# Ninth gate and up pair of a gated MLP as seven block products, with its weight sums formed in DRAM

## The chip, the cores and the metric

The kernel runs on one core of one Trainium2 chip. The metric is the device time of one execution in microseconds (us); the time before is 644.41 us, the median of three runs (644.31 to 644.88). The engines named below are TensorE (PE in the profile, with its weight loads as PEld), VectorE (DVE), ScalarE (ACT), GpSimd (POOL), and SyncE (SP), whose queue issues most transfers.

## The reference

One decoder layer on 512 tokens of width 1024: forgetting attention with 16 heads, a layer norm, a gated MLP, a second layer norm and a gated embedding. Only the MLP matters here:

```python
def conv_ffn(x, w_up, conv_w, conv_b, w_down):
    u, g = jnp.split(x @ w_up, [FFN_DIM], axis=-1)          # FFN_DIM = 2816
    g = causal_dwconv(g, conv_w, conv_b)                    # 3 taps along the tokens
    return (jax.nn.gelu(g, approximate=False) * u) @ w_down
```

## The kernel before

Every float32 product is made of three matmuls in a reduced float32 format. Each operand is split into a high part (a rounded copy, by ACT) and a low part (the operand less the high part, by DVE); the products high by high, high by low and low by high are summed in PSUM (`three`, line 147). The class `Weights` (line 64) holds a list of weight units of up to 128 x 1024 elements in the order of their use. A unit is loaded by the SP queue into one of four `raw` buffers (every fifth unit into a spare one), perhaps combined with other blocks by its `make` function on DVE, and then cut into its `whi` and `wlo` tiles, of which there are five of each (lines 123 and 129). `W.get(u, 4)` cuts all units up to the fourth behind `u`, so DVE and ACT receive the work on a weight four units ahead of its use.

The 2816 columns of the MLP are 22 blocks `f` of 128. Two neighbouring blocks are a pair `j`. A plain pair multiplies all eight k-blocks by all 512 tokens, for gate and up of both blocks (`up`, line 789): 4 x 8 x 3 = 96 matmuls of 512 columns. A pair in `UP_PAIRS` is treated as a 2 x 2 block product (two halves of k by the two blocks `f`, and two halves of the tokens), with seven instead of eight products (`up_step`, line 836). Its steps 0, 1, 2 and 3 hold two, two, two and one product for gate and the same for up: 7 x 2 x 4 x 3 = 168 matmuls of 256 columns. This needs sums of weight blocks. For the pairs 3 to 7 (`KEPT`) DVE forms them during attention (`keep_sums`, line 488) and they wait in DRAM tiles `kept`; for the pairs 2 and 9 the `make` functions `t12`, `t3`, `t4` (lines 199 to 226) form them when needed (line 208, 209, 216 and 224). Pair 8 is plain. Such a pair has seven weight units where a plain one has four.

The output product with `w_down` is also done by seven products, on three groups of three pairs (`down`, line 910): its generator yields after each of its 12 chunks, which are spread through the pairs of the next part by `CHUNKS` (line 32) in the calls of `between` (line 961). In phase `ua` the chunks 0, 1 and 2 use the first, second and third pair of the group before, their operands A11 and A12. When a chain is complete, `give` (line 934) adds its PSUM banks to `y` in SBUF (lines 703 and 705). The six banks of the chains (`y`, `z`, `x`, two of each) come from a pool of six; two more banks belong to another tag.

The operands of `down` come from a pair's products: `operand_sums` (line 892) forms four sums on DVE, and `operand_parts` (line 904) cuts the blocks A, B and S into high and low parts (for pair 8 the tiles `a8`, `b8`, `s8`). For a pair whose successor is in `APART` this is put off: the sums are called inside the second step 0 of the next pair (`amid`, line 865), and the parts right after that step (lines 988 to 994). Pair 8 is not in `APART`, so pair 7's operands, and pair 8's own, are made directly at the end of their pairs (line 1030). From block 2 on, `tc.manual_schedule` (line 971) fixes the order of the instructions of DVE and ACT as the code gives it. The order on PE and the queues is chosen by the framework when the program is built.

Part 3 (from line 957) holds the pairs 9 and 10. With the chunk counts (2, 1) repeated, the order of pair 9 in the code is: step 0 of gate, chunks 0 and 1, step 0 of up, chunk 2, step 1 of gate and of up, chunks 3 and 4, step 2 of both, chunk 5, step 3 of both. Beside the pairs, `gate_sums` (line 277) issues one accumulating transfer for each block from 6 on, on the POOL queue, each behind a tiny ACT copy (line 282) and a tiny POOL copy (line 283): they form the weight sums of the last gate in DRAM tiles `gt`.

Of the kernel before, what the change touches and what calls it, by code (L numbers as in the profile page):

```python
# [40 lines left out]
HALF = S // 2  # L41
ALPHA = 2.0 ** 0.25
EPS = 1e-5
# [99 lines left out]
def trunk_layer(ctx: ExitStack, tc: tile.TileContext, xT, x2d, pT, w0, wqk, wv1, wv2, bf, wo, wup, cwb,  # L143
# [10 lines left out]

    base = ctx.enter_context(tc.tile_pool(name="base", bufs=1))
    psum = ctx.enter_context(tc.tile_pool(name="psum", bufs=6, space=bass.MemoryType.PSUM))
    turns = itertools.cycle(BANKS)

    def bank(name, tag=None):

        tag = tag or next(turns)
        return psum.tile([P, 512], F32, tag=tag, name=name, bufs={"six": 6, "two": 2}[tag])

    def half_rows(w, k0, n, cols):
        return w[k0 * P:(k0 + n) * P, cols * 512:(cols + 1) * 512].rearrange("(k p) c -> p k c", p=P)
# [30 lines left out]

        return aside[0][:, i, :]

    def t12(b11, i):
        def make(t):  # L200
            if t is None:
                to = side(i)
                if len(b11.shape) == 3:
                    to = to.rearrange("p (a b) -> p a b", b=P)
                nc.sync.dma_start(to, b11)
                return None
            t1, t2 = t[:, :512], side(i)
            nc.vector.tensor_sub(t1, t1, t2)
            nc.vector.tensor_sub(t2, t[:, 512:], t1)
            return [t1, t2]  # L210
        return make

    def t3(t):
        if t is None:
            return None
        nc.vector.tensor_sub(t[:, :512], t[:, 512:], t[:, :512])  # L216
        return [t]

    def t4(i, n=2):
        def make(t):  # L220
            if t is None:
                return None
            v = t[:, :n * 512]
            nc.vector.tensor_sub(v, v, aside[0][:, i:i + n, :].rearrange("p a b -> p (a b)"))
            return [v]
        return make

# [12 lines left out]
    def up_units(j):  # L240

        f0, f1 = 2 * j, 2 * j + 1
        if j in KEPT:
# [8 lines left out]
        return (lambda q: unit(f0, q), lambda q: unit(f1, q, t12(wup[f0, 1 - q][:, :4], 3 + q)),  # L252
                lambda q: unit(f1, q, t3),
                lambda q: W.add([(wup[f0, 1 - i][:, 4:], 512) for i in range(2)], make=t4(3)))

    dram = ctx.enter_context(tc.tile_pool(name="dram", bufs=1, space=bass.MemoryType.DRAM))
    kept = {(j, q): dram.tile([P, 4, 512], F32, name=f"kept{j}_{q}") for j in KEPT for q in range(2)}


    gq = {f"t{n}": dram.tile([P, 4, 512], F32, name=f"gt{n}") for n in range(1, 5)}  # L260

    steps = itertools.count(16)

    def quad(g, k, n):
        src = gq[g] if g in gq else half_rows(wg, 4 * int(g[1]) - 4, 4, int(g[2]) - 1)
        return src[:, k:k + n, :]
# [7 lines left out]
                    nc.gpsimd.dma_start(quad(to, k, 2), quad(src, k, 2))  # L274
        yield

    def gate_sums():

        for to, src in (("t1", "b12"), ("t2", "t1"), ("t4", "t2"), ("t3", "b12")):
            for k in range(4):  # L280
                m = next(steps)
                nc.scalar.activation(small[:, m:m + 1], zeros[:, :1], AF.Copy)  # L282
                with tc.issue_after(nc.gpsimd.tensor_copy(small[:, m + 32:m + 33], small[:, m:m + 1]).ins):  # L283
                    nc.gpsimd.dma_start(quad(to, k, 1), quad(src, k, 1), accum_op=ALU.add)
                yield

    u_up, u_dn = {}, [[] for _ in PAIRS]
    for part in range(4):
# [180 lines left out]
            nc.gpsimd.memset(t[:, :P].bitcast(F32), 0.0)  # L469


    to_keep, in_work, made, last_sum, last_mask = list(kept.items()), [], [], [], []

    def keep_load(queue=nc.sync):

# [12 lines left out]
    def keep_sums(first=last_mask):  # L488

        if in_work:  # L490
            behind = ExitStack()
            if first:
                behind.enter_context(tc.issue_after(first[0]))
            to, ab = in_work.pop()
            b11, b21, b12, b22 = [t[:, c:c + 512] for t in ab for c in (0, 512)]
            nc.vector.tensor_sub(b11, b12, b11)
            nc.vector.tensor_sub(b12, b22, b12)
            nc.vector.tensor_sub(b22, b22, b11)
            last_sum[:] = [nc.vector.tensor_sub(b21, b21, b22).ins]
            behind.close()  # L500
            made.append((to, ab))

# [108 lines left out]

    outs = {}
    acc = {}

    def out_first(k):
        hi, lo = W.get(u_o[0][k // 2])
# [202 lines left out]
    def x_sums():  # L819
        def blk(t, k):  # L820
            return xt[t][:, 4 * k:4 * k + 4, :]

        def s(n, i):
            return sums[n][:, :, i * P:(i + 1) * P]

        for i in range(2):
            nc.vector.tensor_add(s(0, i), blk(2 + i, 0), blk(2 + i, 1))
            nc.vector.tensor_sub(s(1, i), s(0, i), blk(i, 0))
            nc.vector.tensor_sub(s(2, i), blk(i, 0), blk(2 + i, 0))
            nc.vector.tensor_sub(s(3, i), blk(i, 1), s(1, i))  # L830
        for n in range(4):
            k = slice(4 * n, 4 * n + 4)
            nc.scalar.activation(xs[0][:, k, :], sums[n], AF.Copy)
            nc.vector.tensor_sub(xs[1][:, k, :], sums[n], xs[0][:, k, :].bitcast(F32))

    def up_step(j, st, s, E, amid=None):
# [30 lines left out]
        elif st == 1:  # L867
            go(z, 0, True, sn=0)
            go(x, 1, True, sn=1)
            nc.scalar.activation(e[:, S:S + HALF], x, AF.Copy)  # L870
            nc.scalar.activation(e[:, S + HALF:], z, AF.Copy)
            if j in APART:
                nc.scalar.activation(e[:, :HALF], c1, AF.Copy)
        elif st == 2:
            go(z, 1, True, sn=3)
            go(x, 0, True, sn=2)
            nc.vector.tensor_add(e[:, S:], ps, e[:, S:])
# [14 lines left out]
    def operand_sums(E):  # L892


        def e(n):
            return E[:, n * HALF:(n + 1) * HALF]

        a21, a11, a22, a12, s1, s2, s3, s4 = [e(n) for n in range(8)]
        nc.vector.tensor_add(s1, a21, a22)
# [10 lines left out]
    def down(part, ops):  # L910
# [4 lines left out]
        A11, A12, A22, S1, S2, S3, S4 = (0, 0), (0, 1), (1, 0), (2, 0), (2, 1), (2, 2), (2, 3)  # L915
# [37 lines left out]
    before = None  # L953
    pending = []
    beside = gate_sums()
    ordered = ExitStack()
    for part in range(4):
        ops = []
# [5 lines left out]

        for f in range(6 * part, min(6 * part + 6, NF)):
            q, j = f % 2, f // 2
            if f >= 6:
                next(beside)
            if f == 2:

# [287 lines left out]
```

## Time and profile before

| | |
|---|---|
| time, median of three runs | 644.41 us |
| time of the profiled execution | 644.6 us |
| its span (first to last instruction) | 642.9 us |
| granted TensorE clock | 0.999 |
| PE busy | 636.6 us, 99% of the span |
| DVE busy | 540.7 us, 84% |
| ACT busy | 389.4 us, 61% |
| POOL busy | 129.1 us, 20% |

A row of the timeline gives the start in us, the duration, the engine, the line of the code, the operation and its output and inputs; idle time ahead of it stands in brackets with what ended it. A row of the chain of work gives start, duration, engine, the output's name and the number of instructions. A row of the windows gives for a stretch of time its length, then the busy time of PE, PEld, DVE, ACT and POOL with their instructions, the granted clock, the share of DMA time and GB/s. A row of the groups gives the count, the busy time and the mean in ns, and the idle time before. In the chain, `g` and `u` are gate and up, and `x`, `y`, `z` chains of the output product.

### The profile page before, as it was taken

Reading aid. Unit: us, or ns where it says so; the run is one execution under the profiler, and the core shown is the slowest. Engines: PE = TensorE matmul, PEld = TensorE weight load, DVE = VectorE, ACT = ScalarE, POOL = GpSimd, SP = SyncE. Lnnn points to the kernel's source line nnn. Section 1 sums busy time; section 2 is a strip of 40 time slices with the busy share of each in tenths; the row PEclk is TensorE's granted clock in tenths of the full one; section 3 lists DMA queues with packets and bytes.
Section 4 is the critical chain, followed back from the end, with each engine's and each line's share of the span. In section 5 each row is a group of like instructions: output and inputs, shape, how many; then the busy total and the mean of one; then the engine's idle time right before and its main releaser. Section 6 shows DMA issues by size and latency. Waiting matters only on the chain.

```text
span 642.9 us, 10251 instructions
## 1 busy us (share of the span) xinstructions
PE 636.6 (99%) x3707; PEld 562.4 (87%) x3707; DVE 540.7 (84%) x864; ACT 389.4 (61%) x690; POOL 129.1 (20%) x149
## 2 busy tenths in 40 slices
PE   9999999999999999999999999999999999999997
PEld 7899888888888889989999999999988998888886
DVE  7577779988888689857889989999986998599996
ACT  6273787877785316956666566756644455236872
POOL 2000464454456043110000000102020001002001
PEclk9999999999999999999999999999999999999999
DMA  8766634554588777694676868675854774662632
GB/s 316 249 225 211 220 105 166 175 193 152 181 280 295 269 258 204 147 252 137 197 224 154 239 183 275 189 234 168 255 152 123 207 246 100 181 232 73 221 108 98
DMA packets 51666, 126.87 MB, mean 197 GB/s; under 512 B 5088, under 2 KB 8160, under 8 KB 51616
## 3 DMA queue, kind: packets, MB, share of 16 engines
q1 hardware_dynamic: 46384, 111.93, 52.1%
q0 software_dynamic: 5088, 14.16, 11.3%
q8 instruction: 29, 0.48, 0.3%
q14 instruction: 21, 0.17, 0.1%
q10 hardware_dynamic: 144, 0.13, 0.1%
HBM read 111.39 MB, written 20.97 MB: 206 GB/s over the span
## 4 chain that ended last, share of the span: by engine, by line
PE 92%; DVE 4%; issue 1%; DMA 1%; POOL 0%; SPq 0%; ACT 0%; DVEq 0%; POOLq 0%
PE u L152 17%; PE g L152 17%; PE pp L152 13%; PE x L152 8%; PE pl L152 7%; PE pv L152 7%; PE z L152 4%; PE r L152 3%; PE o L600 3%; PE ao L152 3%; PE t L587 3%; PE y L152 2%; PE s L550 2%; PE s L552 2%; PE p L152 1%
## 5 line engine op out<-in xcount | busy, mean ns | idle before, releaser
L123 ACT ACTIVATE whi<-raw 128x1024 fp32r<-128x1024 f32 (+4 forms) x131 | 128.9, 987 | 92.2 <-PE pv L152 18.4
L129 DVE TENSOR_TENSOR wlo<-raw,whi 128x1024 fp32r<-128x1024 f32 (+4 forms) x126 | 141.7, 1129 | 26.7 <-ACT whi L123 26.0
L574 POOL TENSOR_SCALAR pr<-pr,rl 128x128 f32<-128x128 f32 (+1 forms) x64 | 75.6, 1197 | 74.7 <-DVE rl L570 74.7
L283 POOL COPY neghalf<-neghalf 128x1 f32<-128x1 f32 x16 | 9.6, 601 | 244.3 <-ACT neghalf L282 244.3
L152 PE MATMUL g<-x1h,whi 128*128 128x256 f32 (+1 forms) x164 | 51.7, 315 | 0.0
L152 PE MATMUL g<-x1l,whi 128*128 128x256 f32 (+1 forms) x164 | 51.6, 315 | 0.0
L152 PE MATMUL g<-x1h,wlo 128*128 128x256 f32 (+1 forms) x164 | 51.5, 314 | 0.0
L152 PE MATMUL pp<-xh,wlo 128*128 128x512 f32 (+1 forms) x130 | 50.5, 390 | 0.0
L152 PE MATMUL pp<-xh,whi 128*128 128x512 f32 (+1 forms) x130 | 50.5, 388 | 0.1
L152 PE MATMUL pp<-xl,whi 128*128 128x512 f32 (+1 forms) x130 | 50.4, 388 | 0.0
L152 PE MATMUL u<-x1l,whi 128*128 128x256 f32 (+1 forms) x156 | 50.1, 321 | 0.0
L152 PE MATMUL u<-x1h,wlo 128*128 128x256 f32 (+1 forms) x156 | 50.1, 321 | 0.0
L152 PE MATMUL u<-x1h,whi 128*128 128x256 f32 (+1 forms) x156 | 50.1, 321 | 0.0
L566 ACT ACTIVATE pr<-s,nm 128x128 f32<-128x128 f32 (+1 forms) x64 | 33.6, 527 | 11.8 <-DVE nm L562 11.7
L152 PEld LDWEIGHTS g<-x1h,whi 128*128 128x128 f32 x164 | 31.2, 191 | 2.4 <-issue 0.4
L152 PEld LDWEIGHTS g<-x1l,whi 128*128 128x128 f32 x164 | 31.2, 190 | 2.1
L152 PEld LDWEIGHTS g<-x1h,wlo 128*128 128x128 f32 x164 | 31.2, 190 | 1.9
L123 ACT ACTIVATE whi<-side 128x512 fp32r<-128x512 f32 (+1 forms) x32 | 26.4, 828 | 9.3 <-DVE side L216 3.8
L152 PEld LDWEIGHTS u<-x1l,whi 128*128 128x128 f32 x156 | 29.7, 190 | 2.4
L152 PEld LDWEIGHTS u<-x1h,whi 128*128 128x128 f32 x156 | 29.7, 190 | 2.3
L152 PE MATMUL g<-xsh,wlo 128*128 128x256 f32 x112 | 31.7, 283 | 0.0
L152 PE MATMUL u<-xsh,whi 128*128 128x256 f32 x112 | 31.7, 283 | 0.0
(637 smaller groups left out, 1927.7 us busy)
## 6 DMA issues: line engine op xcount, KB each, us to landing
raw<-wup SPq DMA_DIRECT2D x30, 512.0 KB, 4.8
raw<-wdn SPq DMA_DIRECT2D x26, 512.0 KB, 4.8
raw<-wqk SPq DMA_DIRECT2D x14, 512.0 KB, 3.9
ka<-wup SPq DMA_DIRECT2D x10, 512.0 KB
kb<-wup SPq DMA_DIRECT2D x10, 512.0 KB, 4.3
kept<-kb SPq DMA_DIRECT2D x9, 512.0 KB, 3.4
kept<-ka SPq DMA_DIRECT2D x9, 512.0 KB
raw<-wo SPq DMA_DIRECT2D x8, 512.0 KB, 5.1
```

The lines of the kernel that those rows point to most:

```text
L123: self.nc.scalar.activation(hi[:, c:e], piece, AF.Copy)
L129: self.nc.vector.tensor_sub(lo[:, c:e], piece, hi[:, c:e].bitcast(F32))
L152: nc.tensor.matmul(ps, lhsT, rhs, start=start and n == 0, stop=stop and n == 2, skip_group_check=on)
L283: with tc.issue_after(nc.gpsimd.tensor_copy(small[:, m + 32:m + 33], small[:, m:m + 1]).ins):
L550: nc.tensor.matmul(ps[:, :n], QA[:, q], KA[:, :n], start=True, stop=False)
L552: nc.tensor.matmul(ps[:, :n], qb[0:68, q], kb[0:68, :n], start=False, stop=True)
L566: nc.scalar.activation(pr[:, off:off + w], ps[:, :w], AF.Exp, bias=nm[:, i:i + 1], scale=-1.0, accum_out=ls[:, i:i + 1])
L574: nc.gpsimd.tensor_scalar_mul(pr[:, off:off + w], pr[:, off:off + w], rl[:, i:i + 1])
L587: nc.tensor.transpose(ps[:, w:w + P], pr[:, o:o + P], ident)
L600: nc.tensor.matmul(ps[:, q0:], V[:, j, h], p[:, o:o + w], start=j == 0 and n == 0, stop=j == NT - 1 and n == 1)
```

## The change

Pair 8 joins `UP_PAIRS` and becomes seven products. Its weight sums are not made by DVE. Four transfers during the heads 2 and 3 copy the raw blocks to two DRAM tiles (`up_copies`, on the SP queue), and eight accumulating transfers (`sums_beside`, on the POOL queue) turn them into the sums. [...] The eight transfers come ahead of the sixteen of the last gate, one per block from 4 to 14, two from 15 to 20, one at 21 (`BESIDE`).

Pairs 8 and 9 join `APART`: the operands of pair 7 are made in the second step 0 of pair 8, and those of pair 8 in the second step 0 of pair 9. `CHUNKS` of part 2 takes the pattern of part 1, so its third pair (8) has the counts 0, 1, 2, 1 where it had 1, 1, 1, 1. The `y` chains are no longer added to `y` after every part: their two banks are kept and accumulate through three parts, and `give` adds them once. For this the pool of six banks is split in four and two, taken in the turn four, four, two. `operand_sums` does its four subtractions and sums in three operations.

```diff
-CHUNKS = (None, (1,) * 8 + (0, 1, 2, 1), (1,) * 12, (2, 1) * 4)
-UP_PAIRS = (2, 3, 4, 5, 6, 7, 9)
+CHUNKS = (None,) + ((1,) * 8 + (0, 1, 2, 1),) * 2 + ((2, 1) * 4,)
+UP_PAIRS = (2, 3, 4, 5, 6, 7, 8, 9)
+IN_DRAM = (8,)
+BESIDE = (0,) * 4 + (1,) * 11 + (2,) * 6 + (1,)
-APART = (2, 3, 4, 5, 6, 7)
+APART = (2, 3, 4, 5, 6, 7, 8, 9)
+COPIES = (2, 3)
...
-    turns = itertools.cycle(BANKS)
+    turns, sixth = itertools.cycle(BANKS), itertools.cycle(("four", "four", "duo"))
...
+        if tag == "six":
+            tag = next(sixth)
...
+    def up_copies():
+        for j in IN_DRAM:
+            for q in range(2):
+                for n in range(2):
+                    nc.sync.dma_start(kept[j, q][:, 2 * n:2 * n + 2, :].rearrange("p a (k b) -> p (a k) b", b=P),
+                                      wup[2 * j + n, 1 - q])
+                    yield
+    def sums_beside():
+        def blocks(j):
+            for to, src in ((0, None), (2, None), (3, 0), (1, 3)):
...
+        for to, src in itertools.chain(*[blocks(j) for j in IN_DRAM], gates()):
+            m = next(steps)
+            nc.scalar.activation(small[:, m:m + 1], zeros[:, :1], AF.Copy)
+            with tc.issue_after(nc.gpsimd.tensor_copy(small[:, m + 32:m + 33], small[:, m:m + 1]).ins):
+                nc.gpsimd.dma_start(to, src, accum_op=ALU.add)
+            yield
...
+        for _ in range(2 if h in COPIES else 0):
+            next(copies)
...
-        nc.vector.tensor_sub(s2, s1, a11)
-        nc.vector.tensor_sub(s3, a11, a21)
+        nc.vector.tensor_sub(e3[:, 5:7, :], e3[:, 0:5:4, :], a11.unsqueeze(1).to_broadcast([P, 2, HALF]))
         nc.vector.tensor_sub(s4, a12, s2)
...
-        acc = {(b, i): bank(f"{b}{part}{i}", "six") for b in "yzx" for i in range(2)}
-        seen, opened = set(), set()
+        acc = {(b, i): bank(f"{b}{part}{i}", "four") for b in "zx" for i in range(2)}
+        if not lasting:
+            lasting.update({("y", i): bank(f"y{i}", "duo") for i in range(2)})
+        acc.update(lasting)
+        seen, opened = set(), {("y", i) for i in range(2) if part}
...
-                        give(b, half, c)
+                        if b != "y" or part == len(PAIRS) - 1:
+                            give(b, half, c)
```

More of the change, by code (lines that the diff above doesn't have):

```diff
@@ L156, in trunk_layer @@
     psum = ctx.enter_context(tc.tile_pool(name="psum", bufs=6, space=bass.MemoryType.PSUM))
-    turns = itertools.cycle(BANKS)
+    turns, sixth = itertools.cycle(BANKS), itertools.cycle(("four", "four", "duo"))
     def bank(name, tag=None):
         tag = tag or next(turns)
-        return psum.tile([P, 512], F32, tag=tag, name=name, bufs={"six": 6, "two": 2}[tag])
+        if tag == "six":
+            tag = next(sixth)
+        return psum.tile([P, 512], F32, tag=tag, name=name, bufs={"four": 4, "duo": 2, "two": 2}[tag])
     def half_rows(w, k0, n, cols):
@@ L215, in t3, with up_t3, t4 @@
             return None
-        nc.vector.tensor_sub(t[:, :512], t[:, 512:], t[:, :512])
+        nc.vector.tensor_sub(t[:, :512], t[:, :512], t[:, 512:])
         return [t]
-    def t4(i, n=2):
+    def up_t3(t):
+        if t is None:
+            return None
+        nc.vector.tensor_add(t[:, :512], t[:, 512:], t[:, :512])
+        return [t]
+    def t4(i, n=2, op=nc.vector.tensor_sub):
         def make(t):
@@ L250, in unit @@
             return W.add(wup[f, 1 - q], inner=P, make=make, by_dma=make is None and j in DMA_PAIRS)
-        return (lambda q: unit(f0, q), lambda q: unit(f1, q, t12(wup[f0, 1 - q][:, :4], 3 + q)),
-                lambda q: unit(f1, q, t3),
-                lambda q: W.add([(wup[f0, 1 - i][:, 4:], 512) for i in range(2)], make=t4(3)))
+        add = nc.vector.tensor_add
+        return (lambda q: unit(f0, q), lambda q: unit(f1, q, t12(wup[f0, 1 - q][:, :4], 3 + q, add)),
+                lambda q: unit(f1, q, up_t3),
+                lambda q: W.add([(wup[f0, 1 - i][:, 4:], 512) for i in range(2)], make=t4(3, op=add)))
     dram = ctx.enter_context(tc.tile_pool(name="dram", bufs=1, space=bass.MemoryType.DRAM))
-    kept = {(j, q): dram.tile([P, 4, 512], F32, name=f"kept{j}_{q}") for j in KEPT for q in range(2)}
+    kept = {(j, q): dram.tile([P, 4, 512], F32, name=f"kept{j}_{q}")
+            for j in KEPT + IN_DRAM for q in range(2)}
     gq = {f"t{n}": dram.tile([P, 4, 512], F32, name=f"gt{n}") for n in range(1, 5)}
-    steps = itertools.count(16)
+    steps = itertools.cycle(range(16, 32))
     def quad(g, k, n):
@@ L275, in gate_copies, with gates @@
         yield
[L277 to L285, printed above, removed]
+    def up_copies():
[8 more added lines that the diff above has]
+            for to, src in ((0, None), (2, None), (3, 0), (1, 3)):
+                for q in range(2):
+                    t = kept[j, q]
+                    if src is None:
+                        yield (t[:, to, :].rearrange("p (k b) -> p k b", b=P),
+                               wup[2 * j + 1, 1 - q][:, 2 * to:2 * to + 4])
+                    else:
+                        yield t[:, to, :], t[:, src, :]
+        def gates():
+            for to, src in (("t1", "b12"), ("t2", "t1"), ("t4", "t2"), ("t3", "b12")):
+                for k in range(4):
+                    yield quad(to, k, 1), quad(src, k, 1)
+        for to, src in itertools.chain(*[blocks(j) for j in IN_DRAM], gates()):
[4 more added lines that the diff above has]
+            yield
     u_up, u_dn = {}, [[] for _ in PAIRS]
@@ L469, in trunk_layer @@
             nc.gpsimd.memset(t[:, :P].bitcast(F32), 0.0)
-    to_keep, in_work, made, last_sum, last_mask = list(kept.items()), [], [], [], []
+    to_keep = [(k, t) for k, t in kept.items() if k[0] in KEPT]
+    in_work, made, last_sum, last_mask = [], [], [], []
     def keep_load(queue=nc.sync):
@@ L495, in keep_sums @@
             b11, b21, b12, b22 = [t[:, c:c + 512] for t in ab for c in (0, 512)]
[L496 to L499, printed above, removed]
+            nc.vector.tensor_add(b11, b12, b11)
+            nc.vector.tensor_add(b12, b22, b12)
+            nc.vector.tensor_add(b22, b22, b11)
+            last_sum[:] = [nc.vector.tensor_add(b21, b21, b22).ins]
             behind.close()
@@ L613, in trunk_layer @@
     acc = {}
+    copies = up_copies()
     def out_first(k):
@@ L896, in e @@
             return E[:, n * HALF:(n + 1) * HALF]
-        a21, a11, a22, a12, s1, s2, s3, s4 = [e(n) for n in range(8)]
+        a21, a11, a22, a12, s1, s3, s2, s4 = [e(n) for n in range(8)]
+        e3 = E.rearrange("p (a b) -> p a b", b=HALF)
         nc.vector.tensor_add(s1, a21, a22)
-        nc.vector.tensor_sub(s2, s1, a11)
-        nc.vector.tensor_sub(s3, a11, a21)
+        nc.vector.tensor_sub(e3[:, 5:7, :], e3[:, 0:5:4, :], a11.unsqueeze(1).to_broadcast([P, 2, HALF]))
         nc.vector.tensor_sub(s4, a12, s2)
@@ L949, in down @@
                     for b, half, c in done:
-                        give(b, half, c)
+                        if b != "y" or part == len(PAIRS) - 1:
+                            give(b, half, c)
                 yield
-    before = None
+    before, lasting = None, {}
     pending = []
-    beside = gate_sums()
+    beside = sums_beside()
     ordered = ExitStack()
@@ L966, in trunk_layer @@
             q, j = f % 2, f // 2
-            if f >= 6:
+            for _ in range(BESIDE[f]):
                 next(beside)
```

24 lines of the change are left out of this document (12 added, 12 removed).

## The prediction

> **What bounds the kernel now.** I read the page's head and its chain first, to see which engine sets the end.
>
> ```profile
> span 642.9 us, 10251 instructions
> PE 636.6 (99%) x3707; PEld 562.4 (87%) x3707; DVE 540.7 (84%) x864; ACT 389.4 (61%) x690; POOL 129.1 (20%) x149
> PE 92%; DVE 4%; issue 1%; DMA 1%; POOL 0%; SPq 0%; ACT 0%; DVEq 0%; POOLq 0%
> ```
>
> PE is busy 99% of the span and is 92% of the chain. A change pays by what it takes off PE, as long as nothing new comes late for PE. DVE at 84% is a mean, so I then read the windows of the MLP's stages.
>
> ```profile
> 375.00:402.00 27.00, 27.00 (x200) 25.76 (x199) 23.84 (x34) 17.26 (x30) 2.44 (x4) 1.00 0.75 221
> 464.00:493.00 29.00, 29.00 (x130) 23.77 (x129) 20.78 (x31) 12.66 (x20) 3.80 (x4) 1.00 0.57 168
> 493.00:530.00 37.00, 37.00 (x243) 33.97 (x242) 36.63 (x54) 20.54 (x33) 2.19 (x4) 1.00 0.68 195
> ```
>
> These are the pairs 5, 8 and 9. The third busy time, after PE and PEld, is DVE's. In pair 9, whose weight sums DVE makes on the spot, DVE has 36.63 of 37.00 us: there it is as full as PE. Pair 8, the one that changes, leaves DVE 8.2 us free (29.00 - 20.78), and so in kind will the plain pair 10. So pair 8 can take more DVE work, while whatever the change pushes from pair 8 into pair 9 meets an engine with no room.
>
> **The gain on PE.** The chain shows every step of pairs 5 and 8.
>
> ```profile
> 374.79 2.88 PE g L152 x24
> 401.81 2.88 PE g L152 x24
> 464.05 5.47 PE g L152 x24
> 472.24 5.44 PE u L152 x24
> 479.04 5.65 PE g L152 x24
> 486.05 5.44 PE u L152 x24
> 492.85 2.87 PE g L152 x24
> ```
>
> Pair 8 has four groups of 24 matmuls of 512 columns: 5.47 + 5.44 + 5.65 + 5.44 = 22.00 us. As seven products it has 168 matmuls of 256 columns, seven groups of 24 at 2.87 or 2.88 us, 20.1 us. So the products alone give 1.9 us. Halving the columns does not quite halve the time (2.87 against half of 5.44, 2.72); an eighth fewer products would otherwise give 2.75.
>
> The page "TensorE: Matmul & The Clock Gate" of the Trainium skill, section "Part 2", gives as isolated gap N/2.4 + 2.5 ns; as an estimate that is 216 and 109 ns, and a gain of 2.4 us. Here a 512-column matmul takes 5.44/24 = 227 ns and a 256-column one 120, so the rows decide for the smaller gain.
>
> Pair 5 is a better template than this sum: seven products, sums kept in DRAM, third of its part, and with the chunk counts 0, 1, 2, 1 that pair 8 now gets. It goes from 374.79 to 401.81, 27.02 us; pair 8 now goes from 464.05 to 492.85, 28.80. Both hold four output chunks. The gain is 28.80 - 27.02 = 1.78 us, and I take this one. That pair 5 runs without a gap on PE with 23.84 us of DVE in 27 is also the reason to expect no stall inside the new pair 8, which brings three more weight units to cut.
>
> **What is pushed into pair 9.** Now pair 8's operands are made at once, and DVE is nearly idle before them; pair 5 shows how a seven-product pair ends on DVE.
>
> ```profile
> 406.46 0.69 DVE L812 TENSOR_TENSOR E<-a,E 128x512 f32<-128x512 f32 x1 [0.76 <-ACT a L811]
> 411.44 0.42 DVE L899 TENSOR_TENSOR E<-E 128x256 f32<-128x256 f32 x1
> 412.91 0.42 DVE L866 TENSOR_TENSOR side<-u,side 128x256 f32<-128x256 f32 x1
> 413.25 0.68 DVE L908 TENSOR_TENSOR a5l<-E,a5h 128x512 fp32r<-128x512 f32 x1
> 491.60 0.69 DVE L812 TENSOR_TENSOR E<-a,u 128x512 f32<-128x512 f32 x1 [2.20 <-PE u L152]
> 493.80 0.68 DVE L908 TENSOR_TENSOR a8l<-E,a8h 128x512 fp32r<-128x512 f32 x1
> 498.48 0.68 DVE L208 TENSOR_TENSOR side<-side 128x512 f32<-128x512 f32 x1
> 508.88 0.42 DVE L866 TENSOR_TENSOR E<-u,side 128x256 f32<-128x256 f32 x1
> ```
>
> DVE finishes the plain pair 8 at 492.29, 0.6 us before pair 9 starts on PE (492.85). It finishes pair 5 at 407.15, 5.3 us after pair 6 started (401.81). So in the changed kernel DVE enters pair 9 at 5.3 us after its start. Its order is fixed by the code: next comes what now runs from 498.48 to 508.88 without a hole, 10.4 us (weight sums and low parts for four units ahead, and one addition). Only then come the operand sums, which take 412.91 - 411.44 = 1.5 us, the addition of line 866 (0.3 us to the next start), and a8l (0.7). Sum: 5.3 + 10.4 + 1.5 + 0.3 + 0.7 = 18.2 us into pair 9. Fusing two sums is worth 0.1 of this, since one operation of 512 columns takes 0.7 where two of 256 take 0.42 each.
>
> And who needs a8l?
>
> ```profile
> 501.19 2.87 PE u L152 x24
> 504.07 1.39 PE x L152 x6
> 518.03 2.87 PE g L152 x24
> 529.41 5.47 PE g L152 x24
> ```
>
> Chunk 2, the third of this part, is the first that uses pair 8's operands. It stands at 504.07, 11.2 us into pair 9. Now a8l is there at 494.5; in the changed kernel it comes 18.2 - 11.2 = 7.0 us too late for this place. That is the whole risk of the change. Queued behind a waiting chunk 2 are, on PE, step 1 of pair 9 (two groups of 2.87 us), and on DVE the additions of the chunk's chains.
>
> PE's order is not fixed by the code, however. The chain shows what the framework does when an operand comes late:
>
> ```profile
> 96.46 1.15 PE pp L152 x5
> 97.61 0.44 PE s L550
> 98.05 0.24 PE s L552
> ```
>
> These are the scores of one head. The code calls all of them ahead of the projection, yet five projection matmuls stand before the last two scores. So later work that is ready is put ahead of late work when the program is built, and it came out within 0.2 us of the right place (0.44 against 0.24 us for the score that waited). In pair 9 the work for this is there: step 1 of gate and of up (2 x 2.87) and chunk 3 (2.75) make 8.5 us, and their low parts are done by 15.7 us, before a8l. That covers the 7.0.
>
> What is late next is step 2 of pair 9.
>
> ```profile
> 495.01 1.23 DVE L908 TENSOR_TENSOR s8l<-E,s8h 128x1024 fp32r<-128x1024 f32 x1 [0.19 <-ACT s8h L907]
> 509.21 0.68 DVE L216 TENSOR_TENSOR raw<-raw 128x512 f32<-128x512 f32 x1
> 514.01 1.22 DVE L129 TENSOR_TENSOR wlo<-raw,whi 128x1024 fp32r<-128x1024 f32 x1
> ```
>
> The low part of its first unit ends at 515.2 now, 2.8 us before its use at 518.03. In the changed kernel b8l (0.3) and s8l (1.1 to the next start) follow a8l, then the same work as from 509.21 to 515.23, 6.0 us: ready at 18.2 + 1.4 + 6.0 = 25.6 us, needed at 518.03 - 492.85 = 25.2 whatever the order of the work ahead. PE waits 0.4 us here. Later units gain: DVE has less to do per unit from there, and the plain pair 10 lets it catch up. Pair 8's and pair 9's products share one tile E, so pair 9's first writes to it, the ACT copies of step 1, wait for s8l (19.6 us); step 2 overwrites their PSUM source only from 25.2 on, so nothing is lost there. With 0.2 for the place of chunk 2, I take 0.6 us of waits.
>
> **The rest, which I cost at nothing.**
>
> ```profile
> gt<-wg POOLq DMA_DIRECT2D x8, 512.0 KB, 5.5
> gt<-gt POOLq DMA_DIRECT2D x8, 256.0 KB, 5.2
> ka<-wup SPq DMA_DIRECT2D x10, 512.0 KB
> 106.00:150.00 44.00, 44.00 (x237) 37.53 (x236) 37.87 (x88) 33.53 (x79) 22.87 (x21) 1.00 0.59 202
> 480.56 1.23 DVE L129 TENSOR_TENSOR wlo<-side,whi 128x1024 fp32r<-128x1024 f32 x1 [0.26 <-ACT whi L123]
> 480.68 1.15 POOL L283 COPY neghalf<-neghalf 128x1 f32<-128x1 f32 x1 [7.75 <-ACT neghalf L282]
> 496.07 0.20 POOL L283 COPY neghalf<-neghalf 128x1 f32<-128x1 f32 x1 [13.48 <-ACT neghalf L282]
> L705 DVE TENSOR_TENSOR y<-y,y 128x512 f32<-128x512 f32 x6 | 3.8, 679 | 0.0
> L703 DVE SCALAR_TENSOR_TENSOR y<-y,x 128x512 f32<-128x512 f32 x6 | 3.8, 678 | 0.0
> ```
>
> The four copies from DRAM to DRAM go on SP's queue at the heads 2 and 3. Queued behind them are the loads of the next projection's weights and the small transfers of `stack`, for which the scores wait. Every other even head already puts four transfers of 512 KB on this queue, and with them PE is busy 44.00 of 44.00 us. Head 2 puts none. A copy of this size lands in 5.5 us on POOL's queue; so nothing is the likely price, and one exposed copy (5.5) the upper bound.
>
> The eight accumulating transfers take about 5.2 us each and end with block 11, in pair 5 (to 401.81). Pair 8 starts at 464.05 and loads at most a pair ahead, so they are done some 30 us early. Each brings a small ACT and a small POOL copy. The copy takes 0.20 us alone and 1.15 when it meets a DVE operation that started just before; the DVE operation keeps its 1.23.
>
> The page "SBUF — State Buffer" of the Trainium skill, section "Who interferes with whom", says that DVE with two SBUF inputs and a GpSimd read exclude each other, the later one waiting whole. The trace agrees: POOL waited 1.15 us. By that rule DVE could lose 0.2 us per copy, in pair 9 for two more of them.
>
> The y chains in PSUM take four of the six additions of 0.68 us off DVE, in the pairs 4 and 7, where DVE is not late, so PE gains nothing. The `scalar_tensor_tensor` costs what an addition does (678 and 679 ns). The split of the six banks in four and two leaves each bank six turns between its uses. No row shows it; I bound it between a gain of 0.3 and a loss of 0.5 and take nothing.
>
> **Sum.** On the profiled execution (644.6 us, with 1.7 around the span): 644.6 - 1.8 + 0.6 = 643.4. The median stands 0.2 lower, so 643.2 us, 0.18% under 644.41. A measurement of this kernel tells about 0.2% (1.3 us) from no change.
>
> **The rivals.** Full gain: the waits do not appear, because the framework places the work well and DVE is half a microsecond earlier than I sum. Then 644.41 - 1.8 = 642.6. For it: the gapless chain of all pairs now. Against it: DVE's 36.63 of 37.00. Chance 0.22.
>
> Slower: chunk 2 stays in its place on PE. Then PE stands 7.0 us at 11.2 us into pair 9, DVE catches up in that time, and nothing else is late: 644.41 - 1.8 + 7.0 = 649.6. It decides against the change as soon as the wait is over 1.8 us. For it: within the MLP of the pairs the trace shows PE only in the code's order. Against it: the scores above. Chance 0.13 for the whole wait, and 0.15 for part of it (3 to 6 us, 645.6 to 648.6), if the framework reckons DVE faster than it is and puts chunk 2 ahead of one step instead of three.
>
> The copies or the bank split expose something in attention, worth about the gain: 644.4. For it: four transfers more on a queue that the scores depend on. Against it: the heads with `keep_load`. Chance 0.08. That the seven products do not appear I exclude; the code path is the one of pair 5.
>
> **The numbers.** My forecast has 0.42: waits from 0.2 to 1.5 us, 642.8 to 644.1. Of it 0.14 (waits under 0.5) lies beyond 0.2%. Faster is 0.22 + 0.14 = 0.36; slower is 0.13 + 0.15 = 0.28; the same is the rest, 0.36. The range goes from 642.3 (full gain and the banks' 0.3) to 648.0; it leaves out most of the whole wait of 7.0 and the end of the partial ones, about 0.17.
>
> **What would show it.** Right: pair 8 takes about 27.0 us on the chain; pair 9 starts about 491; a8l ends about 18 us after that; PE rows of `g` and `u` of step 1 stand ahead of the third x, y chunk; a hole of under 1 us ahead of step 2. Wrong: a hole of several us on PE ended by a8l or a8h (the slower rival); a hole in the heads 2 to 4; DVE ready with a8l by 12 us (then my sum of DVE's queue is wrong); or a gain over 2 us.

## The result, and the profile after

The changed kernel takes 649.81 us (median of four runs, 648.22 to 650.25) where the kernel before takes 644.44: a ratio of 1.0077, 95% interval 1.0062 to 1.0092. It is slower by 5.4 us, outside the range of the prediction. The profiled execution took 649.89 us. The head of its page, engines and chain:

```profile
span 648.2 us, 10455 instructions
PE 637.0 (98%) x3779; PEld 564.9 (87%) x3779; DVE 543.9 (84%) x858; ACT 395.7 (61%) x715; POOL 139.0 (21%) x165
PE 77%; DVE 12%; DMA 5%; ACT 2%; issue 2%; SPq 0%; ACTq 0%; DVEq 0%
```

The span has grown by 5.3 us and PE's busy time by only 0.4. PE's share of the chain has fallen from 92% to 77%, and DVE and DMA, 5% before, hold 17% of it: there are holes on PE now that end on data. The view of the waits, for PE, names them (engine, tile and line, what was waited for, us in total, times, longest). First all of the kernel before, then the longest of the changed one, without the 1.1 us at the start that both have:

```profile
PE warm L339 <- DVE zeros L335: 1.1, 1, 1.1
PE pv L152 <- DVE wlo L129: 0.3, 1, 0.3
PE nt L728 <- DVE y L720: 0.2, 1, 0.2
```

```profile
PE u L158 <- DVE E L920: 1.6, 1, 1.6
PE x L158 <- ACT a8h L950: 1.3, 1, 1.3
PE g L158 <- ACT E L924: 0.8, 2, 0.4
PE u L158 <- DVE side L909: 0.8, 1, 0.8
PE s L590 <- DVE o L647: 0.6, 1, 0.6
PE pv L158 <- DVE QB L575: 0.4, 1, 0.4
```

Of the changed kernel's, only the second and the fourth are in pair 9, where the prediction looked for holes. The first and half of the third are in pair 8 itself, the other half between the pairs 6 and 7, the last two in attention. The windows of the pairs 5, 8 and 9:

```profile
376.46:403.48 27.02, 27.02 (x200) 25.78 (x199) 23.95 (x32) 17.42 (x30) 2.44 (x4) 1.00 0.80 224
466.37:495.81 29.44, 27.44 (x200) 25.79 (x198) 23.97 (x32) 17.97 (x33) 4.51 (x8) 1.00 0.87 229
495.81:535.07 39.26, 37.23 (x240) 33.73 (x241) 38.19 (x56) 22.45 (x41) 5.42 (x8) 1.00 0.72 199
```

Pair 8 has the same 200 matmuls as pair 5 and the same 32 DVE operations in the same DVE time (23.97 and 23.95 us), and still takes 2.42 us longer, with PE idle for 2.00. So it isn't more work that stops it. What differs beside PE is POOL with eight instructions instead of four, ACT with 33 instead of 30 (17.97 and 17.42 us), and a DMA share of 0.87 instead of 0.80.

The table takes from the timeline of PE the start of pair 2 (its first `g` matmul; what lies ahead is attention, layer norm and the pairs 0 and 1), and the lengths of the last pairs, each to the next one's first `g` or, for pair 10, to the first `r` of the last gate (us). The lower rows are experiments, below.

| kernel | pair 2 starts | pair 6 | pair 7 | pair 8 | pair 9 | pair 10 | span |
|---|---|---|---|---|---|---|---|
| before | 292.24 | 31.12 | 31.12 | 28.80 | 36.55 | 34.03 | 642.9 |
| after | 294.07 | 31.68 | 31.21 | 29.44 | 39.26 | 34.03 | 648.2 |
| e3, last gate's transfers left out | 293.75 | 31.12 | 31.12 | 27.02 | 38.10 | 34.03 | 643.7 |
| e7, transfers early | 293.57 | 31.12 | 31.12 | 27.02 | 38.10 | 34.03 | 643.5 |
| e10, and six banks whole | 292.88 | 31.12 | 31.12 | 27.02 | 38.12 | 34.03 | 642.8 |
| e12, and pair 9's sums in DRAM | 303.25 | 31.12 | 31.12 | 27.02 | 37.00 | 34.02 | 652.3 |

The difference of 5.3 us is thus 1.83 ahead of pair 2, 0.65 in the pairs 6 and 7, 0.64 in pair 8, 2.71 in pair 9, and -0.5 behind the first `r` (which no run explains).

How the hole in pair 8 comes about can be followed through four engines of the changed kernel's timeline:

```profile
478.97 0.82 POOL L323 DMA_DIRECT2D gt<-gt  x1 [0.30 <-issue]
479.74 0.99 POOL L323 DMA_DIRECT2D gt<-gt  x1
479.78 0.38 SPq L99 DMA_DIRECT2D raw<-wdn  x1
490.79 1.06 ACT L129 ACTIVATE whi<-raw 128x1024 fp32r<-128x1024 f32 x1 [4.62 <-PE x L158]
491.88 1.23 DVE L135 TENSOR_TENSOR wlo<-raw,whi 128x1024 fp32r<-128x1024 f32 x1 [3.67 <-ACT whi L129]
493.02 0.68 DVE L920 TENSOR_TENSOR E<-E,u 128x512 f32<-128x512 f32 x1
493.75 0.39 PE L158 MATMUL u<-x1h,whi 128*128 128x256 f32 x1 [1.65 <-DVE E L920]
```

Two accumulating transfers of the last gate's sums are issued at 478.97 and 479.74, and right with the second one SP issues the load of an output weight. Its high part starts only at 490.79, 11 us later, and its low part at 491.88. (The bracket of the high part names a matmul that ended at the same moment. It isn't the cause: in e7, below, the same cut starts 2.75 us ahead of the first matmul of that chunk.) DVE stands idle for 3.67 us ahead of that low part. Behind it, in the fixed order of DVE, is the addition of step 2 (line 920), which reads the PSUM bank that step 3 writes: PE waits 1.65 us for it. The weight is cut four units ahead of its use; it is its place in DVE's order that hurts.

### The profile page after: what moved, and what is told of

It reads as the page before. It is cut to its first block, busy times and chain, and to the rows that moved or that the text cites. A ratio compares the mean times of both kernels' runs of the same rounds, so it can differ in the third digit from the quotient of the medians.

```text
span 648.2 us, 10455 instructions
## 1 busy us (share of the span) xinstructions
PE 637.0 (98%) x3779; PEld 564.9 (87%) x3779; DVE 543.9 (84%) x858; ACT 395.7 (61%) x715; POOL 139.0 (21%) x165
## 4 chain that ended last, share of the span: by engine, by line
PE 77%; DVE 12%; DMA 5%; ACT 2%; issue 2%; SPq 0%; ACTq 0%; DVEq 0%
PE u L158 13%; PE g L158 13%; PE pp L158 11%; PE pl L158 7%; PE x L158 5%; PE pv L158 5%; DVE wlo L135 4%; PE r L158 3%; PE ap L158 3%; PE ao L158 3%; PE o L640 3%; PE z L158 3%; DMA side<-wdn 2%; PE t L627 2%; PE s L590 2%
## 5 line engine op out<-in xcount | busy, mean ns | idle before, releaser
L129 ACT ACTIVATE whi<-raw 128x1024 fp32r<-128x1024 f32 (+4 forms) x134 | 131.8, 988 | 97.3 <-PE pv L158 18.5
L135 DVE TENSOR_TENSOR wlo<-raw,whi 128x1024 fp32r<-128x1024 f32 (+4 forms) x129 | 145.3, 1132 | 26.5 <-ACT whi L129 25.8
L322 POOL COPY neghalf<-neghalf 128x1 f32<-128x1 f32 x24 | 13.4, 559 | 241.1 <-ACT neghalf L321 241.1
L158 PE MATMUL g<-x1l,whi 128*128 128x256 f32 (+1 forms) x160 | 48.7, 304 | 0.0
L158 PE MATMUL u<-xsh,whi 128*128 128x256 f32 x128 | 36.3, 284 | 0.8 <-DVE side L909 0.8
L158 PE MATMUL u<-xsh,wlo 128*128 128x256 f32 x128 | 36.2, 283 | 0.0
L158 PE MATMUL u<-xsl,whi 128*128 128x256 f32 x128 | 36.2, 283 | 0.0
L158 PE MATMUL g<-xsh,wlo 128*128 128x256 f32 x128 | 36.2, 283 | 0.0
L158 PE MATMUL g<-xsl,whi 128*128 128x256 f32 x128 | 36.2, 283 | 0.0
L158 PE MATMUL g<-xsh,whi 128*128 128x256 f32 x128 | 36.1, 282 | 0.0
```

The lines of the kernel that those rows point to most:

```text
L129: self.nc.scalar.activation(hi[:, c:e], piece, AF.Copy)
L135: self.nc.vector.tensor_sub(lo[:, c:e], piece, hi[:, c:e].bitcast(F32))
L158: nc.tensor.matmul(ps, lhsT, rhs, start=start and n == 0, stop=stop and n == 2, skip_group_check=on)
```

## The experiments

All kernels are compared with the kernel before on the same chip; the ratio is one of means, intervals are 95%. Two experiments set side by side by their medians can come from different chips, where the kernel before has medians from 644.20 to 644.60 us. The ideas, with their letters: A, the split of the six banks costs time in attention; B, the four copies do; C, the transfers hold up weight loads, in pair 8 above all; D, the seven units of pair 8 are too much to load in any case; E, the cost of pair 9 comes from putting pair 8's operands off; F, DVE has simply too much work from the end of pair 8 to step 2 of pair 9, in whatever order.

**The bank split alone (e1).** The kernel before, with the split and the kept `y` chains, nothing else:

```diff
-    turns = itertools.cycle(BANKS)
+    turns, sixth = itertools.cycle(BANKS), itertools.cycle(("four", "four", "duo"))
...
+        acc.update(lasting)
```

> The kernel before with one part of the change alone: the six PSUM banks split in four and two, and the y chains kept in PSUM over three parts. The changed kernel reaches the first seven-product pair's step 1 at 299.98 us instead of 298.15, so 1.8 us are lost before any step that pair 8 touches. Theory A (the bank split makes the scores, projections and values of attention wait for each other): this kernel loses 1.5 to 2.5 us ahead of the pairs, and its time is 646 to 647. Theory B (the four copies on the SP queue do it): attention ends where it does in the kernel before, and the time is within 0.5 us of 644.4. In the pairs 3 to 10 neither theory expects a change on PE.

It took 646.11 us, ratio 1.0030 (1.0019 to 1.0041), about 1.9 us more, and pair 2 starts 1.44 us later. The windows from the start to pair 2, first of before, then of e1:

```profile
0.00:292.24 292.24, 290.52 (x1600) 251.95 (x1600) 232.02 (x442) 185.40 (x366) 97.78 (x107) 1.00 0.67 215
```

```profile
0.00:293.68 293.68, 291.85 (x1600) 253.21 (x1600) 232.07 (x442) 185.35 (x366) 99.56 (x107) 1.00 0.67 214
```

A holds, and the two lines show its form. Both have 1600 matmuls; PE's idle time grows by 0.11 us (from 1.72 to 1.83), its busy time by 1.33. The timelines show that the other turn of the banks leads the framework to another order of the matmuls: ahead of pair 2, e1, the changed kernel and every other kernel with the split have one and the same order, and the kernel before, e2, e8 and e10 another; the two differ in 114 of some 1600 places. In the first, pair 2 starts at 293.57 to 294.76 us, in the second at 291.86 to 292.88, which is 1.8 us apart in the mean. Whether the order itself costs that, or waits too short to stand out as idle, the runs do not tell: the profile models the ends of the matmuls, so a short wait can lie within the busy time.

**The copies alone (e2).** The kernel before with four copies of the same size at the heads 2 and 3, into tiles that nothing reads:

```diff
+        for _ in range(2 if h in (2, 3) else 0):
+            next(copies)
```

> The kernel before with only the four copies of pair 8's blocks added, at the heads 2 and 3, to DRAM tiles that nobody reads. Theory A (the bank split costs attention 1.8 us): nothing measurable, 644.4 within 0.5. Theory B (the copies): 645.5 to 647, with the loss ahead of head 6 and none after it.

644.01 us, ratio 0.9991 (0.9982 to 1.0001); pair 2 starts at 292.19. B falls.

**The last gate's transfers left out (e3).** Sixteen of the 24 accumulating transfers are gone from the changed kernel, and with them the weight sums of the last gate:

```diff
-BESIDE = (0,) * 4 + (1,) * 11 + (2,) * 6 + (1,)
+BESIDE = (0,) * 4 + (1,) * 8 + (0,) * 10
...
-        for to, src in itertools.chain(*[blocks(j) for j in IN_DRAM], gates()):
+        for to, src in itertools.chain(*[blocks(j) for j in IN_DRAM]):
```

> The changed kernel without the sixteen accumulating transfers of the last gate (its weight sums are left out, so the last gate computes with unsummed blocks); the eight of pair 8 stay. In the changed kernel PE waits 2.3 us inside pair 8, on a chain of work that leads back to a weight load which took 8.8 us to land while two accumulating transfers were on their way. Theory C (the doubled rate of these transfers in blocks 15 to 20 holds the loads up): pair 8 takes 27.0 to 27.3 us instead of 29.4, the 0.55 us ahead of pair 7 are gone too, and the time is 646.5 to 647.3. Theory D (the seven units of pair 8 alone are too much to load, 3.5 MB instead of 2): pair 8 still takes 28.5 or more and the time is over 648.5.

645.72 us, ratio 1.0017 (1.0007 to 1.0026). The holes in pair 8 and ahead of pair 7 are gone, pair 8 takes 27.02 us, the length of pair 5 to the hundredth, and pair 9 is 1.16 us shorter, since DVE enters it earlier. C holds and D falls; the time is even below the range that I had given for C.

**The operands of pair 8 at once (e4), and the same without the last gate's transfers (e5).**

```diff
-APART = (2, 3, 4, 5, 6, 7, 8, 9)
+APART = (2, 3, 4, 5, 6, 7, 8)
```

This is e4; e5 has the lines of e3 as well.

> The changed kernel with pair 9 taken out of APART, so that pair 8's operands are made at the end of pair 8 as in the kernel before, and not behind the weight sums of pair 9. Theory E (chunk 2 of the output product waits for a8 in pair 9, and step 1 of up for the addition behind the operand sums): pair 9 takes 36.6 to 37.5 us instead of 39.3, and the time is 647.5 to 648.3. Rival F (DVE is simply full in pair 9, so the work that is moved forward delays the weight units of step 1 and 2 by as much): pair 9 takes 38.5 or more, with the waits ahead of steps 1 and 2 on low parts of weights, and the time is over 649.

> The changed kernel without the sixteen transfers of the last gate (its sums are left out) and with pair 8's operands made at the end of pair 8. Without these transfers pair 8 takes 27.0 us, but pair 9 still 38.1 instead of the 36.55 of the kernel before. Theory E (the 1.55 us are the wait of chunk 2 and of step 1 for work behind pair 8's operand sums): pair 9 takes 36.6 to 37.0 and the time is 644.1 to 644.8. Rival F (DVE is full in pair 9, and the sums made at once push the weight units back by the same amount): pair 9 takes 37.8 to 38.6, PE waits on low parts of weights, and the time is 645.3 to 646.3.

e4 took 649.31 us, ratio 1.0078 (1.0052 to 1.0103), with pair 9 at 39.12 us; e5 645.83, ratio 1.0020 (1.0010 to 1.0029), with 38.44. The put-off is not the cause; E falls. PE's waits in pair 9 of e4:

```profile
PE z L158 <- DVE wlo L135: 1.0, 1, 1.0
PE x L158 <- DVE wlo L135: 0.8, 1, 0.8
```

With the operands first, the chunks wait for the low parts of their weights: DVE's queue is as long, only another item in it is late. Both kernels come out as F had it.

**Chunks later (e6).** The third chunk of the last part comes behind step 2:

```diff
-CHUNKS = (None,) + ((1,) * 8 + (0, 1, 2, 1),) * 2 + ((2, 1) * 4,)
+CHUNKS = (None,) + ((1,) * 8 + (0, 1, 2, 1),) * 2 + ((1,) * 4 + (2,) * 4,)
```

> The changed kernel with the twelve output chunks of part 3 dealt as 1, 1, 1, 1, 2, 2, 2, 2 instead of 2, 1, 2, 1, 2, 1, 2, 1: pair 9 gets four and the plain pair 10 eight. Pairs 9 and 10 together take 70.6 us in the kernel before and 73.3 in the changed one. If DVE's fullness in pair 9 is the cause of the waits there (F), two output chunks with their sums and low parts moved to pair 10, where DVE has room, and chunk 2 placed behind step 1, leave no wait of over 0.3 us in pair 9 even behind a late pair 8: together 70.6 to 71.2, and the time is 647.2 to 648.0. If instead the weights' arrival sets the pace (a full load queue), the waits only move: together 72.5 or more, and the time is over 649.

649.46 us, ratio 1.0084 (1.0067 to 1.0102). My expectation for F missed: the pairs 9 and 10 together take 73.23 us, after 73.29, and that is what I had written down for the rival, by which the waits only move. The wait on a8h is gone, but the one on line 909 is 1.0 us instead of 0.8, and a new one of 0.6 comes in pair 10, for the bank of an `x` chain. Pair 8 is late in e6 as before; in e8, below, where it isn't, the same chunks leave no wait in pair 9. So e6 does not speak for F. What does are e4 and e5, and e11 and e12 below.

**Transfers early (e7).** The same 24 transfers, two per block in the blocks 4 to 9 and one from 10 on:

```diff
-BESIDE = (0,) * 4 + (1,) * 11 + (2,) * 6 + (1,)
+BESIDE = (0,) * 4 + (2,) * 6 + (1,) * 12
```

> The changed kernel with the same 24 accumulating transfers dealt otherwise: two in each of the blocks 4 to 9, one from 10 to 21, so that none of the pairs 5 to 10 has more than the kernel before had. Theory C (two per block, in the loads of pairs 7 and 8, made those land late): pair 8 takes 27.0 to 27.4 us, the time is 646.0 to 647.2, and a wait may appear in pairs 2 to 4, at most 0.6. Rival (it is the number of transfers and not their place): the same 2 us turn up in the pairs 2 to 4 and the time is over 648.5.

645.74 us, ratio 1.0021 (1.0012 to 1.0030), again a little below the range that I had given for C. By the medians, 649.81 to 645.74, the line is worth 4.1 us, by the ratios 3.6. The rows that answer to those of pair 8 above, in e7:

```profile
477.33 0.82 POOL L323 DMA_DIRECT2D gt<-gt  x1
478.36 0.38 SPq L99 DMA_DIRECT2D raw<-wdn  x1
485.24 1.06 ACT L129 ACTIVATE whi<-raw 128x1024 fp32r<-128x1024 f32 x1 [0.50 <-ACT whi L129]
486.70 1.22 DVE L135 TENSOR_TENSOR wlo<-raw,whi 128x1024 fp32r<-128x1024 f32 x1
488.19 0.69 DVE L920 TENSOR_TENSOR E<-E,u 128x512 f32<-128x512 f32 x1 [0.27 <-PE u L158]
487.99 0.40 PE L158 MATMUL x<-whi,b5h 128*128 128x512 f32 x1
```

From the issue of the load to the low part it is 8.3 us where it was 12.1, and the addition of line 920 waits for PE now, not PE for it. The section "Queues, rings and completion order" of the page "DMA: Bandwidth & Descriptors" of the Trainium skill says that a DMA engine takes packets from its queues in turn; by that rule transfers on POOL's queue lengthen loads on SP's, and the trace agrees (12.1 us with two transfers just ahead, 8.3 with one).

In the blocks 4 to 9, where e7 has two transfers per block, PE has no hole: doubling as such does no harm there. Two waits are left in e7's MLP, both in pair 9:

```profile
PE u L158 <- DVE side L909: 0.8, 1, 0.8
PE x L158 <- ACT a8h L950: 0.2, 1, 0.2
```

**Doubled in pair 8 alone (e9).**

```diff
-BESIDE = (0,) * 4 + (2,) * 6 + (1,) * 12
+BESIDE = (0,) * 4 + (2,) * 6 + (1,) * 6 + (2, 2, 1, 1, 0, 0)
```

> The kernel with the sums early (e7), with the same 24 transfers, but the blocks 16 and 17 (pair 8) take two each and the blocks 20 and 21 none. Theory C, in the form that the rate in the pair itself decides (two transfers per block beside the loads of a pair with seven units): pair 8 goes from 27.02 us back to 28.5 to 29.5, and the time from 645.7 to 647.5 or more. Rival: the doubling alone does no harm, and what held up the loads of pair 8 in the changed kernel was which transfers came there; then pair 8 stays near 27.0 us and the time at 645.7.

646.94 us, ratio 1.0041 (1.0028 to 1.0055), 1.2 us more than e7. Pair 8 takes 27.31 us, far below the 28.5 I expected; the rest shows as a wait of 1.3 us on a8h in pair 9, which takes 39.24 as in the changed kernel. So the doubling in pair 8 delays DVE, and most of it is paid one pair later. It gives back only part of the 4.1 us. The changed kernel doubles six blocks, 15 to 20, and e9 only two of them, with other transfers in pair 8; which of these makes the remainder isn't separated.

**Six banks whole (e8, e10).** Both are e7 with the six banks in one pool again and `y` added after every part; e8 has the chunks of e6 as well.

```diff
-        acc = {(b, i): bank(f"{b}{part}{i}", "four") for b in "zx" for i in range(2)}
+        acc = {(b, i): bank(f"{b}{part}{i}", "six") for b in "yzx" for i in range(2)}
```

> The changed kernel with three things put otherwise: the pool of six banks whole and the y chains added after each part as in the kernel before, the transfers dealt as two in the blocks 4 to 9 and one after, and the chunks of part 3 as 1, 1, 1, 1, 2, 2, 2, 2. If the three causes (bank split 1.6 us, transfers about 2.9, the full DVE in pair 9 about 1.5 to 2.7) are separate and complete, the seven products of pair 8 keep their gain: 642.4 to 643.2. If the causes overlap or another is left, 643.8 to 645.5.

> The kernel of e8 with the chunk counts (2, 1) of the last part as in the changed kernel. The later chunks gained nothing in e6 (pairs 9 and 10 took 73.2 us with them and 73.3 without) and brought a wait of 0.56 us in pair 10 in e8; so I expect the same time as e8 within 0.5 us, 643.4 to 644.4 us, with the pairs 9 and 10 at 71.6 to 72.3 us. If the later chunks did help once the transfers are out of the way, it comes out over 644.4.

e8 took 643.92 us, ratio 0.9987 (0.9978 to 0.9997); e10 643.85, ratio 0.9993 (0.9984 to 1.0002). The two aren't told apart. The interval of e8 lies just below 1 and that of e10 reaches it, so the gain against the kernel before is small: 0.13% in e8, 0.7 us by the medians (643.92 and 644.59). That lies in the second of the two ranges that I had given for e8: the causes overlap, or another is left. e8's waits on PE, all of them:

```profile
PE warm L376 <- DVE zeros L372: 1.1, 1, 1.1
PE x L158 <- DVE y L746: 0.6, 1, 0.6
```

None is in pair 9, yet the pairs 9 and 10 together take 71.81 us (72.14 in e10, 70.58 in the kernel before): only 0.6 of the 1.23 us is a hole.

e7 and e10 differ in the banks alone: 1.0021 against 0.9993, 0.28% or 1.8 us, as in e1. From pair 2 to the end both take 349.9 us, so all of it lies ahead of pair 2. Of that the two profiles show only 0.69 us (293.57 and 292.88); e10's profiled execution took 644.53 us, 0.7 above its median, so its profile shows less of the gain; the comparison over all kernels under e1 has 1.8.

**Pair 9's sums in DRAM as well (e11, e12).** Both are e10 with eight copies and 32 accumulating transfers, which take the weight sums of pair 9 off DVE.

```diff
-IN_DRAM = (8,)
+IN_DRAM = (8, 9)
-BESIDE = (0,) * 4 + (2,) * 6 + (1,) * 12
+BESIDE = (2,) * 10 + (1,) * 12
-COPIES = (2, 3)
+COPIES = (2, 3, 9, 11)
```

These are the lines of e12; e11 has the copies at the heads 2, 3, 5 and 7 and `BESIDE = (0,) * 3 + (2,) * 13 + (1,) * 6`.

> The kernel of e10, and the weight sums of pair 9 too are formed by transfers (eight copies during four heads, sixteen accumulating transfers ahead of the sixteen of the last gate, two per block from 3 to 15). This takes the sums of t12, t3 and t4 off DVE in pair 9, about eight operations or 5 us. Theory F (DVE is full when it enters pair 9, so about 1.5 us of the gain is lost there): pair 9 goes from about 38.1 to 36.2 to 36.8 us, and the time to 642.0 to 643.0 us, 0.2 to 0.4% under the kernel before. Rival, theory C goes on: the longer doubling (thirteen blocks instead of six) holds up loads in the pairs 5 to 7, each by 0.3 to 0.6 us, and eats this gain: 643.5 to 645 us. If pair 9 still takes 38 us with no holdup elsewhere, theory F falls.

> The kernel of e11 with its transfers placed by what the runs showed so far: two accumulating transfers per block from 0 to 9 and one from 10 to 21, and the four further copies at the heads 9 and 11, not 5 and 7. Theory C together with F: the pairs 5 to 8 go without the holes of e11 (pairs 5 and 8 at 27.0 us, 6 and 7 at 31.1), the hole at 77 us in attention goes, and pair 9 keeps the length of e11 (37.0 us, where e10 has 38.1); so the time is that of e10 less about 1.1 us, 642.3 to 643.3 us. Rival: what held up e11 is the sum of the transfers (eight copies and 32 accumulating ones in all), whatever the place; then the holes come elsewhere, and the time is 645 us or more.

Both were slower: e11 648.12 us, ratio 1.0065 (1.0052 to 1.0078); e12 653.68, ratio 1.0153 (1.0128 to 1.0178). Yet each shows what it was made for. Pair 9 takes 36.99 and 37.00 us, where it took 38.12 in e10: with less work on DVE, its holes are gone and 1.1 of the 1.5 us come back, which is F. 0.44 us stay without a hole. In e11, with two transfers per block up to block 15, the holes are back in the pairs 5, 6 and 8 (27.43, 33.61 and 27.94 us), as the rival had it but larger: 2.5 us in pair 6, where it had at most 0.6. Pair 2 starts 1.2 us later too. Three of the holes in its MLP, from PE's waits:

```profile
PE g L158 <- DVE E L918: 1.1, 1, 1.1
PE g L158 <- ACT E L922: 0.8, 2, 0.6
```

In e12, with the transfers early, the pairs 5 to 8 have no hole (table). But pair 2 starts 10.4 us later than in e10. PE's longest waits there, and the timeline of POOL:

```profile
PE s L588 <- ACT pr L604: 2.8, 1, 2.8
PE nt L769 <- DVE y L761: 2.7, 1, 2.7
PE t L625 <- POOL pr L612: 1.0, 1, 1.0
```

```profile
51.09 0.82 POOL L321 DMA_DIRECT2D kept<-wup  x1 [17.37 <-DMA kept<-wup]
60.73 0.81 POOL L321 DMA_DIRECT2D kept<-wup  x1 [8.83 <-DMA kept<-wup]
...
260.73 0.83 POOL L321 DMA_DIRECT2D kept<-kept  x1 [7.50 <-DMA kept<-wup]
261.30 0.85 POOL L757 TENSOR_TENSOR mv<-mv,neghalf 128x1 f32<-128x1 f32 x1
```

The code calls these transfers beside the blocks of the MLP, but the framework has put some of them at 51 and 61 us, into attention. The four further copies too, called at the heads 9 and 11, are issued from 54.74 to 75.52 us, hardly elsewhere than in e11 (53.52 to 70.34). Two things come of it.

The longest wait looks like C, in attention. Ahead of the scores' `pr`, ACT cuts a weight, and waits for its load, first in e12, then in e10:

```profile
70.04 1.06 ACT L129 ACTIVATE whi<-raw 128x1024 fp32r<-128x1024 f32 x1 [6.89 <-DMA raw<-wqk]
```

```profile
65.31 1.06 ACT L129 ACTIVATE whi<-raw 128x1024 fp32r<-128x1024 f32 x1 [2.22 <-DMA raw<-wqk]
```

The load is issued at 59.23 us in e12 and at 59.53 in e10, so issue to cut takes 10.8 us and not 5.8. In e12 four copies on SP (52.63 to 56.06) stand just ahead of it and four transfers on POOL (60.73 to 62.40) just behind; in e10 there are no copies, and POOL issues two transfers, ahead of the load (57.40 and 58.11). No run separates these.

The other is POOL itself, which stands 17.37, 8.83 and 7.50 us until a transfer into the `kept` tiles has landed. At 51 us it has nothing else to do; at 260.73 the layer norm's operation of 261.30 is queued behind, and the normalised tokens (`nt`) wait for it on PE. The section "Anatomy of one DMA — SWDGE (gpsimd) path" of the page "DMA: Bandwidth & Descriptors" of the Trainium skill says that a transfer's wait is held by the sequencer that issues it, and the trace agrees (the three idle times above stand on POOL).

Idle time is only part of the 10.4 us. The windows up to pair 2, first of e12, then of e10:

```profile
0.00:303.25 303.25, 295.33 (x1599) 255.60 (x1600) 231.96 (x441) 186.92 (x376) 107.63 (x127) 0.98 0.74 228
```

```profile
0.00:292.88 292.88, 291.32 (x1599) 253.18 (x1600) 232.09 (x441) 185.47 (x368) 99.39 (x111) 1.00 0.69 221
```

PE is idle for 7.92 us instead of 1.56, 6.4 more, and busy for 4.0 more. The granted clock accounts for the latter in kind: behind the first of the two long holes, and behind the second, it is 0.50:

```profile
74.00:78.00 4.00, 4.00 (x11) 3.12 (x10) 1.44 (x2) 1.62 (x4) 0.00 (x0) 0.50 0.90 302
264.00:266.00 2.00, 2.00 (x12) 2.00 (x11) 1.97 (x4) 1.01 (x2) 0.00 (x0) 0.50 1.11 74
```

In the changed kernel, whose longest hole in the MLP is 1.65 us, it stays 1.00.

The rival that I had written down, holes elsewhere and 645 us or more, is what came. I had not foreseen where: the transfers are no longer beside the MLP, and in attention they hold up a load and POOL.

## Why the prediction was wrong, step by step

**The gain on PE** was right. Pair 8 takes 27.02 us in e3, e7, e10 and e12, exactly pair 5's time, so the seven products give the 1.78 us. In the changed kernel other terms hide it.

**"The rest, which I cost at nothing"** is the step that failed, in two of its items.

The first: "they are done some 30 us early". I gave the accumulating transfers a deadline of their own and a price for POOL and DVE, and did not ask what they delay. The eight new ones are early. But they push the sixteen of the last gate back, two per block from block 15 on, into the pairs where the weight loads of a seven-product pair and of the output chunks stand close. They were in the diff, and pair 5, my template, has one transfer per block. Measured: 4.1 us by the medians (e7), 3.6 by the ratios; the profiles show 0.65 in the pairs 6 and 7, 2.42 in pair 8 and 1.16 in pair 9.

The second: the bank split, bounded "between a gain of 0.3 and a loss of 0.5". Measured: 1.8 to 1.9 us by the ratios of e1 and of e7 against e10, 1.6 by e1's medians, 1.4 in e1's profile. I reckoned with banks that come free late in an unchanged order; the runs show that PE gets another order, and no bound for that was in the sum.

At nothing I also put the copies, and e2 bears it out. (The 1.15 us of POOL that I called a wait are the whole length of the small copy; against 0.20 alone it waited 0.95.)

**What is pushed into pair 9.** The sum of DVE's queue was right where the transfers are out of the way: in e7 DVE ends pair 8 at 497.75, 5.5 us after pair 9's start at 492.25 (I said 5.3), and a8l ends at 510.60, 18.3 us after it (I said 18.2). In the changed kernel it is 19.5, since DVE comes late from pair 8. The framework did put later work ahead of chunk 2, as I argued. The cover failed in part, though: I counted "step 1 of gate and of up (2 x 2.87) and chunk 3". In the changed kernel:

```profile
511.08 0.73 PE L158 MATMUL x<-whi,a8h 128*128 128x512 f32 x2 [1.27 <-ACT a8h L950]
514.77 0.38 PE L158 MATMUL u<-xsh,whi 128*128 128x256 f32 x1 [0.76 <-DVE side L909]
```

Only step 1 of gate stands ahead of a8h. Step 1 of up writes the bank that the addition of line 909 reads (line 866 before), and that addition stands behind the operand sums on DVE. I had listed it in the queue and not asked who waits for it. My 0.6 us of waits measure 1.55 in pair 9 (38.10 - 36.55, e7): 1.0 of holes, and 0.55 of longer busy time. The framework cuts the chunks into smaller pieces between the steps there; that this costs the 0.55 isn't shown. The hole that I forecast ahead of step 2 is not there.

**The rivals.** Chunk 2 staying in place with a wait of 7.0 us did not happen; its 649.6 us lies near the result by accident. Of the third rival, something exposed in attention, the bank part is real, at about the price of 1.8 us that the rival gave it and several times the bound of 0.5 that I took.

With the measured terms the sum closes, as differences of the same two traces must; what the experiments add is how pair 8 and pair 9 divide. -1.78 for the products, +0.65 and +2.42 for the transfers in the pairs 6 to 8, +1.16 for what they push into pair 9, +1.55 for pair 9 itself, +1.83 ahead of pair 2 and -0.5 at the end make +5.33 us, against 5.3 between the spans.

## What to carry to other kernels

A transfer that is itself early can still cost: ask what shares the DMA engines with it at its time, and which instruction in a fixed order stands behind the load that it delays. Moving work to a queue moved its waits to the engine that issues it (POOL in e12), so the place counts where the framework puts it, not where the code calls it. And a template pair carries over only with everything that stands beside it, the number of background transfers included.

## What the runs showed of the hardware that was not expected

The low part of a weight came 8.3 us after the issue of its 512 KB load on SP's queue in e7, with one accumulating transfer of 256 KB between DRAM tiles issued 1.0 us ahead, and 12.1 us after it in the changed kernel, with two issued within 0.8 us. In e12, holes of 2.78 and 2.67 us on PE were followed by a granted clock of 0.50 (74 to 78 us and 264 to 266 us); a hole of 1.65 us in the changed kernel was not. The same 1600 matmuls ahead of pair 2 took 290.5 us of PE's busy time in one order and 291.9 in another, at a granted clock of 1.00 both times; short waits may be part of that.
